# Six staging buffers for the raw weight loads, in place of three, in a two-layer flow trunk

## Chip, cores and metric

The kernel runs on one core of a Trainium2 chip. The metric is the time of one execution in microseconds of device time; the time before is the median of three runs.

## What is computed

Two layers run over 2048 latent tokens and 256 context tokens, each of width 1024 and in fp32. A layer normalises the tokens, projects them with one wide matrix, mixes the columns in four groups of heads, gates the result, projects it back and adds it to the tokens. Cut to what matters here:

```python
def hybrid_layer(x, ctx, c, c_ctx, norm_w, ada_w, ada_b, w_in, w_out, ...):
    shift_l, scale_l, gate_l = jnp.split(jax.nn.silu(c) @ ada_w + ada_b, 3, axis=-1)
    ...
    h_l = rms_norm(x, norm_w) * (1.0 + scale_l[:, None, :]) + shift_l[:, None, :]
    h_c = rms_norm(ctx, norm_w) * (1.0 + scale_c) + shift_c
    pl = split_proj(h_l @ w_in)
    pc = split_proj(h_c @ w_in)
    a_l, a_c = gla_mixer(...)          # chunked gated linear attention, both directions
    b_l = fourier_mix(...)             # 2-D Fourier mixing
    c_l, c_c = swa_mixer(...)          # banded attention with sink logits
    d_l, d_c = na_mixer(...)           # 2-D neighbourhood attention
    y_l = jnp.concatenate([a_l * jax.nn.silu(pl['a_g']), ..., d_l * jax.nn.silu(pl['d_g'])], axis=-1) @ w_out
    x = x + gate_l[:, None, :] * y_l
    ...
```

## The kernel before

**Tiling.** The 2304 tokens are nine subs of 256 (the first is the context). `w_in` is cut into twelve column chunks of 256 (`av`, `aqk`, `cq`, `ckv`, `dk`, `dv`, `dq`, `bv` and the four gates) and one of 32 (`lr`); `w_out` into four chunks of 256. A chunk has eight blocks of 128 rows.

**Precision by halves.** fp32 values are split into a rounded part and the rest, and a product is made of three fp32r matmuls of 128x256 per block (`mm3`, lines 216 to 222): high by high, high by low and low by high. So each weight chunk has to be split on the chip before it is used, and `load_w` (lines 204 to 214) does this. It takes the tiles `hi` (`whi`) and `lo` (`wlo`), of which there are two each, and then four times, for two blocks of rows each: a raw tile `wraw` (three buffers), its load of 256 KB on the SP queue (L211), the cast into `whi` on ACT (L212), and the subtraction into `wlo` (L213), by turns on DVE and POOL. The cast and the subtraction both read the raw tile, and the buffer is free for another load when the subtraction is done. `load_w_lr` (lines 194 to 202) does the same for the narrow chunk with one load, and takes its raw tile from the same buffers. `whi` and `wlo` come free when the last matmul with a chunk is done; with two of each, one chunk is converted while the matmuls use another.

**Stages.** `trunk` goes through the subs three at a time: `first_chunks` (normalise, then `av`, `lr`, `aqk`), `mix_a` (the forward half of the gated linear attention, `gla_fast`, around the chunks `bv`, `ckv`, `dk`, `dv`, and in places the modulation of a later use, `ada`, whose loads `adaw` are multiplied on DVE at L167), then `gla_bwd`, `fnet`, and `attention`, in which attention items alternate with projections of the remaining chunks and with `out_proj` (output projection; its input `y`, 512 KB, is loaded at L1081 into a single buffer, multiplied on DVE at L1083, cast on ACT at L1084). A projection ends with an eviction from PSUM on ACT: a copy (`ev`, L311, L314, L322) or, for the normalised heads, `normrope`, which squares on ACT (`nsq`, L372) and multiplies on DVE (L376). There are two PSUM tiles `ps`/`pso` for all projections, so the matmuls of the projection after next wait for that eviction.

**The start.** `ada_first` computes the first modulation: nine blocks on DVE (`adaw`, L167) and seven as matmuls on PE (`adp`, `pad`, L154), whose result DVE copies at L155 before the first `h` can be made.

**What sets the order.** The instructions of each engine stand in an order that Tile's scheduler fixes when the program is built; each engine then runs its own list in that order, and an instruction that waits holds all that stand behind it on that engine. The DMAs named here are all issued by SP, in one list too. So another number of buffers may move instructions on every engine.

Of the kernel before, what the change touches and what calls it, by code (L numbers as in the profile page):

```python
# [8 lines left out]
F32 = mybir.dt.float32  # L9
# [9 lines left out]
KB = 8  # L19
# [18 lines left out]
class Kern:  # L38
# [155 lines left out]
    def load_w_lr(self, src):  # L194

        nc = self.nc
        w = self.wp.tile([128, KB, 64], F32R, tag="wlr", name="wlr", bufs=1)
        raw = self.wp.tile([128, 2, 256], F32, tag="wraw", name="wraw", bufs=3).rearrange("p a (b n) -> p (a b) n", n=32)[:, 0:KB]
        nc.sync.dma_start(raw, src)
        nc.scalar.copy(w[:, :, 0:32], raw)  # L200
        nc.vector.tensor_tensor(out=w[:, :, 32:64], in0=raw, in1=w[:, :, 0:32], op=ALU.subtract)
        return w, None

    def load_w(self, src):
        nc = self.nc
        lo = self.wp.tile([128, KB, 256], F32R, tag="wlo", name="wlo", bufs=2)
        hi = self.wp.tile([128, KB, 256], F32R, tag="whi", name="whi", bufs=2)
        for i in range(0, KB, 2):
            k = slice(i, i + 2)
            raw = self.wp.tile([128, 2, 256], F32, tag="wraw", name="wraw", bufs=3)  # L210
            nc.sync.dma_start(raw, src[:, k])  # L211
            nc.scalar.copy(hi[:, k], raw)  # L212
            (nc.gpsimd if i % 4 else nc.vector).tensor_tensor(out=lo[:, k], in0=raw, in1=hi[:, k], op=ALU.subtract)  # L213
        return hi, lo
# [1168 lines left out]
```

## Time and profile before

| | before |
|---|---|
| median of 3 runs | 2963.52 us |
| the runs | 2957.93, 2963.52, 2965.28 us |
| the profiled execution | 2951.03 us |
| its span, first to last instruction | 2949.1 us |
| PE busy in it (matmuls) | 2718.3 us, 92% |
| PE weight loads | 2410.2 us, 82% |
| DVE busy | 1609.3 us, 55% |
| ACT busy | 1070.9 us, 36% |
| POOL busy | 837.3 us, 28% |
| mean granted TensorE clock | 0.959 of 2.4 GHz |
| DMA | 458.00 MB, mean 155 GB/s |

The engines run at the same time, so their busy times do not add up. A timeline row gives the start in us, the length in us, the engine, the line, the operation, output and inputs, shapes, the count of merged instructions, and in brackets how long the engine was idle before it and what ended that. `SPq` is SP's issuing of a DMA, not the transfer itself. `PEclk` is the clock granted to TensorE: 1.00 is 2.4 GHz and 0.50 is 1.2 GHz.

### The profile page before, as it was taken

The page shows a single profiled execution, that of the slowest core. Times are in us where ns is not written, and L with a number is a line of the kernel's source. Part 1 is how long each engine was busy: PE and PEld are TensorE (multiplying, and loading weights), DVE is VectorE, ACT ScalarE, POOL GpSimd, SP SyncE. Part 2 cuts the span into 40 slices and gives each one's busy share as a digit, 9 for nine tenths or more (in the row PEclk, how much of TensorE's full clock was granted, in tenths as well). Part 3 has the DMA queues.
Part 4 walks back from the last instruction along what each step waited for, and adds up shares of the span by engine and source line. Part 5 has one row for each costly group of instructions (what it writes and reads, how often), then busy time and mean ns, then how long its engine had stood idle before and what let it go on. Part 6 is the DMA issues. An engine that isn't in the chain of part 4 may idle for free. (4 is left out here: it accounts for less than half of the span.)

```text
span 2949.1 us, 55777 instructions
## 1 busy us (share of the span) xinstructions
PE 2718.3 (92%) x21206; PEld 2410.2 (82%) x21206; DVE 1609.3 (55%) x3741; ACT 1070.9 (36%) x2344; POOL 837.3 (28%) x922
## 2 busy tenths in 40 slices
PE   5989988988999999999959889999879999999998
PEld 5889878976888778887859889889768888878788
DVE  7554775557355454645484553464483646455543
ACT  3333323322344343344224323334232444444432
POOL 3233222234132121312133332332351313121222
PEclk9999988999999999999979999989999999999999
DMA  8635544245565274554464664333465654456545
GB/s 273 194 108 163 169 136 126 84 145 166 162 192 167 81 215 129 158 157 124 147 193 134 196 185 144 93 111 104 119 190 162 199 164 135 146 163 190 161 149 180
DMA packets 476681, 458.00 MB, mean 155 GB/s; under 512 B 54763, under 2 KB 355565, under 8 KB 476013
## 3 DMA queue, kind: packets, MB, share of 16 engines
q1 hardware_dynamic: 472782, 440.66, 48.9%
q0 software_dynamic: 3616, 13.64, 1.9%
q8 instruction: 170, 2.79, 0.4%
q14 instruction: 113, 0.93, 0.1%
HBM read 339.56 MB, written 114.60 MB: 154 GB/s over the span
## 5 line engine op out<-in xcount | busy, mean ns | idle before, releaser
L220 PE MATMUL ps<-whi,hh 128*128 128x256 f32 x1968 | 586.4, 298 | 34.7 <-ACT hh L258 17.2
L222 PE MATMUL ps<-whi,hl 128*128 128x256 f32 x1968 | 582.0, 296 | 10.2 <-DVE hl L259 10.2
L221 PE MATMUL ps<-wlo,hh 128*128 128x256 f32 x1968 | 580.8, 295 | 6.4 <-PEq L639 6.4
L213 POOL TENSOR_TENSOR wlo<-wraw,whi 128x512 fp32r<-128x512 f32 x208 | 280.8, 1350 | 775.7 <-ACT whi L212 735.1
L220 PEld LDWEIGHTS ps<-whi,hh 128*128 128x128 f32 x1968 | 391.9, 199 | 46.4 <-ACT hh L258 19.0
L220 PE MATMUL ps<-hh,whi 128*128 128x256 f32 x1376 | 402.5, 292 | 5.3 <-ACT ev L311 2.3
L222 PEld LDWEIGHTS ps<-whi,hl 128*128 128x128 f32 x1968 | 391.3, 199 | 18.5 <-DVE hl L259 13.9
L221 PE MATMUL ps<-hl,whi 128*128 128x256 f32 x1376 | 403.3, 293 | 0.0
L222 PE MATMUL ps<-hh,wlo 128*128 128x256 f32 x1376 | 402.4, 292 | 0.0
L221 PEld LDWEIGHTS ps<-wlo,hh 128*128 128x128 f32 x1968 | 392.4, 199 | 11.0 <-issue 8.8
L212 ACT CAST whi<-wraw 128x512 fp32r<-128x512 f32 x416 | 242.3, 620 | 378.5 <-DMA wraw<-w_in 206.9
L844 ACT ACTIVATE S<-S,am 128x641 f32<-128x641 f32 (+5 forms) x272 | 226.1, 831 | 339.1 <-DVE am L836 324.5
L220 PE MATMUL pso<-mh,whi 128*128 128x256 f32 x1088 | 316.7, 291 | 5.3 <-DVE xo L1107 2.9
L222 PE MATMUL pso<-mh,wlo 128*128 128x256 f32 x1088 | 316.2, 291 | 2.3 <-POOL wlo L213 1.8
L221 PE MATMUL pso<-ml,whi 128*128 128x256 f32 x1088 | 315.1, 290 | 0.0
L213 DVE TENSOR_TENSOR wlo<-wraw,whi 128x512 fp32r<-128x512 f32 x208 | 187.9, 907 | 170.9 <-ACT whi L212 163.4
L220 PEld LDWEIGHTS ps<-hh,whi 128*128 128x128 f32 x1376 | 265.9, 193 | 15.2 <-issue 7.9
L222 PEld LDWEIGHTS ps<-hh,wlo 128*128 128x128 f32 x1376 | 265.8, 193 | 15.1 <-issue 14.8
L221 PEld LDWEIGHTS ps<-hl,whi 128*128 128x128 f32 x1376 | 266.0, 193 | 11.4 <-issue 11.0
L830 PE MATMUL pse<-kst,q 64*128 64x256 f32 (+2 forms) x1184 | 246.6, 457 | 13.6 <-DVE am L836 12.5
L191 POOL TENSOR_TENSOR rs<-ms,mhalf 128x8 f32<-128x8 f32 (+2 forms) x140 | 171.3, 1226 | 297.5 <-DVE ms L189 288.6
L862 PE MATMUL ppt<-idn,S 128*128 128x128 f32 x1360 | 243.6, 284 | 10.4 <-DVE pt L872 5.2
(203 smaller groups left out, 4866.4 us busy)
## 6 DMA issues: line engine op xcount, KB each, us to landing
wraw<-w_in SPq DMA_DIRECT2D x288, 256.0 KB
wraw<-w_out SPq DMA_DIRECT2D x128, 256.0 KB
adaw<-ada_w SPq DMA_DIRECT2D x82, 256.0 KB
scr_g<-ev SPq DMA_DIRECT2D x68, 256.0 KB
g<-scr_g SPq DMA_DIRECT2D x34, 512.0 KB
y<-scr_y SPq DMA_DIRECT2D x34, 512.0 KB
bias<-nbias SPq DMA_DIRECT2D x48, 256.0 KB
scr_h<-x SPq DMA_DIRECT2D x22, 512.0 KB
```

The lines of the kernel that those rows point to most:

```text
L191: nc.gpsimd.tensor_tensor(out=rs, in0=ms, in1=self.mhalf.to_broadcast([128, n]), op=ALU.pow)
L212: nc.scalar.copy(hi[:, k], raw)
L213: (nc.gpsimd if i % 4 else nc.vector).tensor_tensor(out=lo[:, k], in0=raw, in1=hi[:, k], op=ALU.subtract)
L220: nc.tensor.matmul(out, ah(k), bh(k), start=(k == 0), stop=False)
L221: nc.tensor.matmul(out, ah(k), bl(k), start=False, stop=False)
L222: nc.tensor.matmul(out, al(k), bh(k), start=False, stop=(k == KB - 1))
L830: nc.tensor.matmul(p[:, lo:hi], q[r], k, start=True, stop=True, tile_position=(64 * o, 0))
L844: nc.scalar.activation(out=S[:, 0:w], in_=S[:, 0:w], func=AF.Exp, scale=-1.0, bias=m[:, 0:1], accum_out=m[:, 1:2])
L862: nc.tensor.transpose(p[:, i], S[:, (c0 + i) * 128:(c0 + i + 1) * 128], self.idn)
```

## The change

The raw tile `wraw` has six buffers in place of three, at both places that take one. Nothing else in the source differs; no operation is added or removed, and no size of a tile or a transfer changes.

```diff
@@ def load_w_lr
-        raw = self.wp.tile([128, 2, 256], F32, tag="wraw", name="wraw", bufs=3).rearrange(...)[:, 0:KB]
+        raw = self.wp.tile([128, 2, 256], F32, tag="wraw", name="wraw", bufs=6).rearrange(...)[:, 0:KB]
@@ def load_w
-            raw = self.wp.tile([128, 2, 256], F32, tag="wraw", name="wraw", bufs=3)
+            raw = self.wp.tile([128, 2, 256], F32, tag="wraw", name="wraw", bufs=6)
```

A load into a raw buffer used to wait for the subtraction three raw tiles back, and now waits for the one six back. The order of the instructions changes with it, at these places.

**ACT, first pass over the third to fifth sub, layer 0: the chunk `aqk` (`whi_2312`, raw tiles 2313 to 2325).** Before:

```order
L212 CAST whi_2312<-wraw_2313 128x512
L212 CAST whi_2312<-wraw_2317 128x512
L212 CAST whi_2312<-wraw_2321 128x512
L461 COPY rec_1843<-po_1874 128x256
L432 COPY ktt_1917<-pk_1914 128x256
L258 CAST hh_2329<-x_2331 128x8x128
L231 ACTIVATE sq_2516<-x_2514 128x1024
L450 COPY P_1925<-psl_1926 128x256
L450 COPY P_1925<-psl_1933 128x128
L212 CAST whi_2312<-wraw_2325 128x512
L450 COPY P_1925<-psl_1938 128x128
```

After:

```order
L212 CAST whi_2312<-wraw_2313 128x512
L212 CAST whi_2312<-wraw_2317 128x512
L212 CAST whi_2312<-wraw_2321 128x512
L212 CAST whi_2312<-wraw_2325 128x512
L450 COPY P_1855<-psl_1868 128x128
```

The fourth cast moves up to the third. Over all 104 chunks, the four casts stand in one piece on ACT in 13 of them before and in 78 now; between the third and the fourth there stood 697 ACT instructions in all, and there are 6 now.

**SP, the end of the second pass over subs, layer 0: the loads of the chunk `av` (raw tiles 4532 to 4544) among the `adaw` loads of `ada`.** Before:

```order
L211 DMA wraw_4532<-w_in 128x512
L211 DMA wraw_4536<-w_in 128x512
L164 DMA adaw_4437<-ada_w 128x512
L211 DMA wraw_4540<-w_in 128x512
L164 DMA adaw_4443<-ada_w 128x512
...
L164 DMA adaw_4491<-ada_w 128x512
L320 DMA scr_vd0<-ev_3743 2x64x256 x2
L164 DMA adaw_4497<-ada_w 128x512
L211 DMA wraw_4544<-w_in 128x512
L199 DMA wraw_4549<-w_lr 128x256
```

After:

```order
L164 DMA adaw_4401<-ada_w 128x512
L211 DMA wraw_4540<-w_in 128x512
L211 DMA wraw_4544<-w_in 128x512
L199 DMA wraw_4549<-w_lr 128x256
L211 DMA wraw_4555<-w_in 128x512
L164 DMA adaw_4407<-ada_w 128x512
```

The fourth load of the chunk, 4544, stood behind `adaw_4497` and now stands ahead of `adaw_4407`, sixteen `adaw` loads earlier.

**SP, the start of the program: the last loads of `ada_first` and the first `x` loads.** Before:

```order
L164 DMA adaw_314<-ada_w 128x512
L211 DMA wraw_435<-w_in 128x512
L152 DMA adp_286<-ada_w0 128x1024
L229 DMA x_329<-xin 128x8x128
L229 DMA x_346<-xin 128x8x128
L229 DMA x_363<-xin 128x8x128
L229 DMA x_380<-xin 128x8x128
```

After:

```order
L229 DMA x_329<-xin 128x8x128
L164 DMA adaw_314<-ada_w 128x512
L229 DMA x_346<-xin 128x8x128
L229 DMA x_363<-xin 128x8x128
L229 DMA x_380<-xin 128x8x128
L152 DMA adp_286<-ada_w0 128x1024
```

The last weights for PE's part of the modulation, `adp_286`, stood ahead of four `x` loads of 512 KB and now stand behind them; the raw weight loads of this piece (427, 431, 435) moved to the front of the list.

## Rows read from the trace of the kernel before

**Rows 1.** The page: busy time of the engines, and the chain that ended last, by line.

```profile
PE 2718.3 (92%) x21206; PEld 2410.2 (82%) x21206; DVE 1609.3 (55%) x3741; ACT 1070.9 (36%) x2344; POOL 837.3 (28%) x922
...
PE pse L830 3%; PE ppt L862 3%; PE py L922 2%; PE ps L222 2%; PE ps L220 2%; PE ps L221 2%; DMA y<-scr_y 2%; PE pso L222 1%; PE pso L220 1%; PE pso L221 1%; DMA brec<-scr_so 1%; DMA wraw<-w_out 1%; PE pab L740 0%; DVE wlo L213 0%; DVE y L1083 0%
```

**Rows 2.** Waits, whole span: who waited for whom, total us, times, longest us.

```profile
ACT whi L212 <- DMA wraw<-w_in: 206.9, 75, 12.6
...
ACT whi L212 <- DMA wraw<-w_out: 94.5, 44, 6.0
...
SPq L211 <- DVE wlo L213: 136.8, 92, 10.4
```

**Rows 3.** Timeline of ACT, 396 to 411 us.

```profile
396.71 1.66 ACT L212 CAST whi<-wraw 128x512 fp32r<-128x512 f32 x3
408.99 0.62 ACT L212 CAST whi<-wraw 128x512 fp32r<-128x512 f32 x1 [10.62 <-DMA wraw<-w_in]
...
409.82 0.59 ACT L372 ACTIVATE nsq<-ps 128x512 f32<-128x512 f32 x1
```

**Rows 4.** Timeline of SP, 396 to 406 us.

```profile
404.00 0.33 SPq L211 DMA_DIRECT2D wraw<-w_in  x1
```

**Rows 5.** Timeline of PE at seven places: the instruction behind each gap.

```profile
143.49 0.36 PE L220 MATMUL ps<-whi,hh 128*128 128x256 f32 x1 [3.83 <-DVE nsq L376]
...
222.60 0.80 PE L435 MATMUL pu<-av,ktt 128*128 128x256 f32 x1 [6.66 <-ACT ktt L432]
...
336.45 0.69 PE L430 MATMUL pk<-idn,A 128*128 128x128 f32 x2 [4.25 <-DVE A L422]
...
413.83 0.58 PE L220 MATMUL ps<-whi,hh 128*128 128x256 f32 x1 [4.86 <-DVE nsq L376]
...
1723.51 0.39 PE L220 MATMUL pso<-mh,whi 128*128 128x256 f32 x1 [1.85 <-ACT whi L212]
...
1752.56 0.58 PE L220 MATMUL ps<-hh,whi 128*128 128x256 f32 x1 [2.31 <-ACT ev L311]
...
1896.39 0.38 PE L220 MATMUL ps<-whi,hh 128*128 128x256 f32 x1 [2.51 <-DVE nsq L376]
```

**Rows 6.** Timeline of ACT just before five of those places.

```profile
140.42 0.62 ACT L212 CAST whi<-wraw 128x512 fp32r<-128x512 f32 x1 [10.05 <-DMA wraw<-w_in]
...
217.79 0.62 ACT L212 CAST whi<-wraw 128x512 fp32r<-128x512 f32 x1 [6.36 <-DMA wraw<-w_in]
...
221.23 1.06 ACT L231 ACTIVATE sq<-x 128x1024 f32<-128x1024 f32 x1 [2.38 <-DMA x<-xin]
...
332.41 0.62 ACT L212 CAST whi<-wraw 128x512 fp32r<-128x512 f32 x1 [5.98 <-DMA wraw<-w_in]
...
1750.03 1.99 ACT L212 CAST whi<-wraw 128x512 fp32r<-128x512 f32 x3 [5.26 <-DMA wraw<-w_in]
...
1892.69 0.62 ACT L212 CAST whi<-wraw 128x512 fp32r<-128x512 f32 x1 [8.15 <-DMA wraw<-w_in]
```

**Rows 7.** Timeline of PE in the last projection, 2931 to 2946 us.

```profile
2933.39 0.39 PE L222 MATMUL pso<-mh,wlo 128*128 128x256 f32 x1 [0.84 <-POOL wlo L213]
...
2941.06 0.39 PE L222 MATMUL pso<-mh,wlo 128*128 128x256 f32 x1 [0.85 <-POOL wlo L213]
```

**Rows 8.** Windows: PE, PEld, DVE, ACT, POOL busy; PEclk, DMA share, GB/s.

```profile
0.00:50.00 50.00, 27.04 (x122) 26.40 (x122) 35.55 (x85) 14.06 (x17) 15.97 (x19) 1.00 0.94 318
...
222.00:232.00 10.00, 9.40 (x42) 8.08 (x43) 3.67 (x6) 2.34 (x6) 5.25 (x5) 0.61 0.34 102
336.00:346.00 10.00, 9.09 (x38) 6.76 (x39) 9.27 (x26) 2.35 (x9) 2.40 (x2) 0.50 0.41 132
408.00:418.00 10.00, 5.14 (x28) 4.62 (x26) 8.69 (x21) 1.58 (x4) 4.14 (x3) 0.66 0.38 126
```

**Rows 9.** Timeline of PE, 38 to 46 us: the last part of the modulation.

```profile
39.28 3.57 PE L154 MATMUL pad<-cs,adp 128*128 128x2 f32 x16 [2.48 <-DMA adp<-ada_w]
```

**Rows 10.** Timeline of DVE, 48 to 52 us: the copy of PE's part.

```profile
49.19 0.17 DVE L155 COPY acc<-pad 128x14 f32<-128x14 f32 x1
```

More of the change, by code (lines that the diff above doesn't have):

```diff
@@ L197, in load_w_lr @@
         w = self.wp.tile([128, KB, 64], F32R, tag="wlr", name="wlr", bufs=1)
-        raw = self.wp.tile([128, 2, 256], F32, tag="wraw", name="wraw", bufs=3).rearrange("p a (b n) -> p (a b) n", n=32)[:, 0:KB]
+        raw = self.wp.tile([128, 2, 256], F32, tag="wraw", name="wraw", bufs=6).rearrange("p a (b n) -> p (a b) n", n=32)[:, 0:KB]
         nc.sync.dma_start(raw, src)
```

## The prediction

> **What bounds the kernel now.** I read the page first. PE is busy for 92% of the span and no other engine for more than 55% [rows 1], so what can be won is PE's idle time, some 230 us (2949.1 less 2718.3), and what a lowered clock costs. A change to the weight path matters only where PE waits for it. The direct waits of PE for weights are a few us in all, so by that view alone there is nothing to win.
>
> The list of waits shows something else. ACT's cast of a raw tile waits for the load of that tile 75 times for `w_in` and 44 times for `w_out`, for 206.9 and 94.5 us, 301.4 together [rows 2]. ACT runs its list in order, so during these waits everything behind the cast stands still: the evictions of PSUM, the copies of the linear attention. So I looked, third, at the timeline of ACT around PE's longer gaps.
>
> The place to learn from is 397 to 414 us. Three casts run in a row at 396.71; the fourth starts at 408.99, after 10.62 us of waiting for its load [rows 3]. SP issued that load only at 404.00 [rows 4], because its buffer was one of three and had to be freed by a subtraction first, and because other loads stood ahead of it on SP. Behind the fourth cast, at 409.82, stands the square `nsq` that empties a PSUM tile [rows 3]; PE, which has two of those, waits 4.86 us until 413.83 for the DVE step behind that square [rows 5]. The same picture comes back at 143, 222, 336, 1752 and 1896 us: a cast on ACT that waited for its load for 10.05, 6.36, 5.98, 5.26 and 8.15 us [rows 6], and a PE gap behind it [rows 5]. At 1723 us PE waits for the cast itself, and in the last projection for the last subtraction [rows 5, 7].
>
> **The change, part by part.** No instruction is added or taken out, and no byte. Three things move.
>
> *The fourth load.* With six buffers the load of a chunk's fourth raw tile waits for a subtraction of the chunk before, not of its own chunk. The order shows it: at the place above it goes out sixteen `adaw` loads earlier, and the four casts of a chunk, in one piece in 13 of 104 chunks, are so in 78. So the wait on the fourth load should mostly vanish, and PE's gaps with it, where nothing else is late:
> - 143 us: the gap of 3.83 goes whole; only `nsq` and its DVE step stood behind the cast [rows 5, 6].
> - 414 us: 4.86, whole, for the same reason [rows 3, 5].
> - 222 us: of 6.66 I take half, 3.33. After the cast ACT waited another 2.38 us for an `x` load [rows 5, 6], and that is what is late next.
> - 336 us: of 4.25 half, 2.13: the exponentials behind the cast also need a DVE step whose time I can't separate [rows 5, 6].
> - 1723, 1752 and 1896 us: 1.85, 2.31 and 2.51, whole; nothing else stands between [rows 5, 6].
> - The last projection: 0.84 and 0.85, 1.69 together [rows 7]. There a chunk serves one sub only, and with six buffers the next chunk's loads are issued while the chunk before is still in use.
>
> Together 3.83 + 4.86 + 3.33 + 2.13 + 1.85 + 2.31 + 2.51 + 1.69 = 22.5 us. Bounds: 28.0 if the two halves go whole, 17.1 if they don't go at all.
>
> *The clock.* Behind three of these gaps the granted clock is 0.61, 0.50 and 0.66 over 10 us [rows 8], that is, at 1.2 GHz for part or all of the time, right after PE had stood idle [rows 5]. If PE had work for that time the loss is 3.9 + 5.0 + 3.4 = 12.3 us. Nothing says that one shorter gap keeps the clock up, as other gaps stand near. I take a quarter, 3.1 us; bounds 0 and 12.3.
>
> *A longer burst on ACT.* Four casts in a row in 65 more chunks (78 less 13) hold what is behind them for one more cast: three take 1.66 us and one 0.62, so one more is 0.52 [rows 3], 33.8 us in all. Of ACT's 301.4 us of waiting [rows 2] I traced 22.5 into PE, 7.5%; by that share the longer bursts cost PE 2.5 us. Bounds 0 and 33.8.
>
> *The start.* `adp_286` now stands behind four `x` loads of 512 KB. At the 318 GB/s of the first 50 us [rows 8] these 2.1 MB take 6.6 us. PE's last part ended at 42.85 (39.28 and 3.57) [rows 9] and DVE read it at 49.19 [rows 10], 6.3 us later. So 0.3 us comes through; bounds 0 and 6.6. The DVE work moved ahead of that copy is only taken from behind it.
>
> *SP.* SP's waits for subtractions ahead of a raw load are 136.8 us for DVE's alone [rows 2]. I cost them at nothing: each load still waits for an earlier subtraction, only a longer way back, and behind it on SP stand stores and loads of `x` and `y`, none of which ends one of the gaps in [rows 5]. If that cover is gone, it is the second rival.
>
> The sum: -22.5 - 3.1 + 2.5 + 0.3 = **-22.8 us**. The profiled execution took 2951.03 us (span 2949.1), so by the sum it would take 2928.2. It lies 12.5 us under the median of the runs; against the median, 2963.5, the sum gives **2940.7 us**, which I forecast, a gain of 0.77%. The forecast's own range: at best 28.0 + 12.3 = 40.3 and some 8 more from waits that I did not trace one by one, 2915; at worst 17.1 - 2.5 - 6.6 = 8.0, 2955.
>
> **The rivals.** *The waits only change their name.* Each gap has a second wait close behind the first, as the `x` load at 221 us [rows 6]; the scheduler has filled the waits with other work, and ACT is busy for 36% only. Then no more is left than PE's direct waits for weights, 1.85 + 1.69 = 3.5 us: 2960.0. That the loads hardly come earlier, because SP itself is late, ends here too. Against it stand the places where nothing but the cast's wait separates PE from its work. The Trainium skill (Perfetto Trace Analysis, Identifying the Most-Contended Engine) tells one to work on the most occupied engine first; by that, easing ACT would leave the time where it is. The gaps on PE that end with ACT's late work speak against reading it so here.
>
> *Slower: the raw loads get in front of loads that the chain waits for.* The `y` loads hold 2% of the chain that ended last [rows 1], 59 us. They have one buffer and can't be issued early. With six raw buffers, up to three more loads of 256 KB may be on their way when a `y` load of 512 KB is issued. One of them ahead of each, at an equal rate, makes it half as long again, 29 us; with the traced gain halved (11 us) the time is 2963.5 + 29 - 11 = 2982. It decides from the point where the `y` loads on the chain grow by 22.8/59, 39%, some 200 KB ahead of each. For it: the chain runs through them in every late `out_proj`. Against it: the same bytes pass in the same stages, and the table's mean is 155 GB/s where the first 50 us ran at 318 [rows 8]. The Trainium skill (DMA: Bandwidth & Descriptors, Issuing engines are not separate DMA queues) says that all DMAs run on the same 16 engines and interleave; by it every load sent earlier takes from those under way. No row of before shows how much.
>
> **How the numbers follow.** About 0.3%, 9 us, is what a measurement of this kernel can tell from no change. The forecast has a chance of 0.62; the first rival 0.24, within 0.3%; the second 0.14. So faster 0.62, same 0.24, slower 0.14. A range from 2915 to 2968 takes in the forecast's own range but for a twentieth at its lower end, and the first rival with 4 us above the median; the second rival is left out.
>
> **What would show it.** Right: ACT's wait for `wraw` falls from 301 us to under 100; at the four places in layer 0 the fourth cast follows the third within a us; PE's gaps before L220 that end with `nsq` shrink; the last projection has no wait for `wlo`. Wrong in the first way: ACT's wait falls, but PE's idle time stays near 230 us, with other releasers. Wrong in the second: the chain's share of `y` loads rises, and DVE's wait for them. If ACT's wait for `wraw` stays near 300 us, the premise is wrong.

## The result and the profile after

The time is **2922.72 us** (median of 4 runs, 2912.85 to 2926.31), against 2961.47 us for the kernel before (4 runs, 2957.93 to 2965.28). The ratio is **0.9878, 95% interval 0.9851 to 0.9904**: faster by 1.2%, 36 us at 2961, where 22.8 us were forecast. The medians themselves lie 38.75 us apart. The sign is as forecast and the time is in the range, but the gain is more than half as large again as the sum, and the runs below show that it came only partly for the reasons given.

The profiled execution took 2924.73 us (span 2922.9), 26.3 less than that of before. This pair shows less than the medians, since the profiled execution of before lies 10 us under its median and that of after 2 us above. From the page of after, busy time and the chain by line, for [rows 1]; below it the core's span and mean granted clock, which were 2949.1 us and 0.959 before:

```profile
PE 2702.4 (92%) x21206; PEld 2404.3 (82%) x21206; DVE 1619.6 (55%) x3741; ACT 1066.4 (36%) x2344; POOL 865.5 (30%) x922
...
PE pse L830 3%; PE ppt L862 3%; PE py L922 2%; PE ps L222 2%; PE ps L220 2%; PE ps L221 2%; DMA y<-scr_y 2%; PE pso L222 1%; PE pso L220 1%; PE pso L221 1%; PE pab L740 1%; DMA wraw<-w_out 0%; DVE ml L1085 0%; DVE S L836 0%; DVE y L1083 0%
```

```profile
core 0: 2922.9 us, clock 0.963
```

PE's idle time (span less busy) went from 230.8 to 220.5 us, only 10.3 less; the other 15.9 us is PE's busy time, for the same 21206 matmuls. Busy time shrinks when more of it runs at 2.4 GHz: a mean of 0.959 over 2949.1 us is (1 - 0.959) x 2 x 2949.1 = 242 us at 1.2 GHz, and 0.963 over 2922.9 us is 216. Where PE has work, half of such time is loss, so by this estimate the clock gives back some 13 us between these two executions (the four of after have 0.960 to 0.964). The Trainium skill (Perfetto Trace Analysis, Identifying the Most-Contended Engine) says that the matmul busy share is not a good measure of how close a kernel is to its roofline; here it stayed at 92% while the time fell by 26 us.

The waits, total us, times, longest us. First ACT's after the change, for [rows 2]:

```profile
ACT wlr L200 <- DMA wraw<-w_lr: 20.5, 5, 6.3
ACT whi L212 <- DMA wraw<-w_in: 14.0, 10, 2.7
ACT whi L212 <- DMA wraw<-w_out: 0.3, 1, 0.3
```

Then two of DVE and PE, before:

```profile
DVE y L1083 <- DMA y<-scr_y: 96.5, 29, 5.5
...
PE ps L220 <- DVE nsq L376: 16.8, 10, 4.9
```

and after:

```profile
DVE y L1083 <- DMA y<-scr_y: 101.6, 28, 6.5
...
PE ps L220 <- DVE nsq L376: 23.5, 11, 9.4
```

ACT's wait for raw tiles of `w_in` and `w_out` fell from 301.4 to 14.3 us, as forecast (the narrow chunk's, at L200, rose from 3.0 to 20.5). But PE's waits for the `nsq` step, which should have shrunk, grew: 16.8 us before, 23.5 after. So 287 us less waiting on ACT stand beside 10.3 us less idling on PE, and the question is whether these waits had anything to do with the gain.

Where the 26 us are, place by place (times of before; a place ends after at the same count of matmuls; us before and after): 138 to 254 us, 116 to 103; 714 to 813, 99 to 92; 1835 to 1951, 116 to 106; from 2848 to the last matmul, 97 to 89. In between some is given back: 1061 to 1150, 89 to 94; 1400 to 1619, 219 to 224; and 2761 to 2848, 87 to 93. The largest piece, of before and then of after (PE, PEld, DVE, ACT, POOL busy; PEclk, DMA share, GB/s):

```profile
138.00:254.00 116.00, 102.19 (x740) 94.52 (x740) 72.27 (x189) 42.43 (x103) 44.22 (x40) 0.90 0.41 126
```

```profile
138.00:241.00 103.00, 94.24 (x746) 88.41 (x745) 71.80 (x174) 42.35 (x98) 42.44 (x40) 0.97 0.45 137
```

Five us of these 13 are PE's idle time (13.8 before, 8.8 after); the rest is busy time, and goes with the clock, 0.90 against 0.97.

### The profile page after: what moved, and what is told of

Same layout as the page of the kernel before. It is cut to its first block, busy times and chain, and to the rows that moved or that the text cites. A ratio compares the mean times of both kernels' runs of the same rounds, so it can differ in the third digit from the quotient of the medians.

```text
span 2922.9 us, 55816 instructions
## 1 busy us (share of the span) xinstructions
PE 2702.4 (92%) x21206; PEld 2404.3 (82%) x21206; DVE 1619.6 (55%) x3741; ACT 1066.4 (36%) x2344; POOL 865.5 (30%) x922
## 5 line engine op out<-in xcount | busy, mean ns | idle before, releaser
L213 POOL TENSOR_TENSOR wlo<-wraw,whi 128x512 fp32r<-128x512 f32 x208 | 304.8, 1478 | 580.0 <-ACT whi L212 520.7
L221 PEld LDWEIGHTS ps<-wlo,hh 128*128 128x128 f32 x1968 | 394.7, 201 | 12.3 <-issue 9.2
L221 PE MATMUL ps<-hl,whi 128*128 128x256 f32 x1376 | 396.9, 288 | 0.0
L212 ACT CAST whi<-wraw 128x512 fp32r<-128x512 f32 x416 | 230.5, 618 | 142.6 <-PE ps L221 43.2
L213 DVE TENSOR_TENSOR wlo<-wraw,whi 128x512 fp32r<-128x512 f32 x208 | 200.7, 972 | 130.3 <-ACT whi L212 118.0
```

The costliest lines, as they stand in the source:

```text
L221: nc.tensor.matmul(out, ah(k), bl(k), start=False, stop=False)
```

## The experiments

All ratios are to runs of the kernel before on the same chip. Idle (span less PE busy time), clock and ACT's wait (for raw tiles, `w_in` and `w_out`) are those of the one profiled execution.

| kernel | ratio, 95% interval | PE idle us | clock | ACT's wait us |
|---|---|---|---|---|
| before | 1 | 230.8 | 0.959 | 301.4 |
| six (the change) | 0.9878, 0.9851 to 0.9904 | 220.5 | 0.963 | 14.3 |
| two (e1) | 1.0113, 1.0082 to 1.0143 | 251.7 | 0.957 | 425.7 |
| four (e2) | 0.9832, 0.9797 to 0.9866 | 199.8 | 0.963 | 43.4 |
| five (e3) | 0.9907, 0.9876 to 0.9938 | 212.9 | 0.961 | 30.5 |
| six, fourth load in its own chunk (e4) | 0.9907, 0.9878 to 0.9936 | 209.6 | 0.963 | 254.6 |
| six, order of three (e5) | 0.9961, 0.9946 to 0.9975 | 221.3 | 0.957 | 274.3 |
| six, order of two (e6) | 1.0028, 1.0016 to 1.0041 | 234.3 | 0.956 | 368.9 |
| six, order of four (e7) | 0.9802, 0.9782 to 0.9821 | 196.3 | 0.966 | 35.7 |
| three, unrelated reordering (e8) | 0.9989, 0.9977 to 1.0002 | 223.4 | 0.955 | 311.1 |
| six, order of three, SP free (e9) | 0.9916, 0.9892 to 0.9939 | 218.4 | 0.957 | 4.6 |
| six, PE's order of three (e10) | 1.0036, 1.0016 to 1.0056 | 245.4 | 0.954 | 14.2 |
| six, order of four, SP free (e11) | 0.9830, 0.9805 to 0.9854 | 197.5 | 0.963 | 16.7 |
| as e9, less modulation work on DVE (e12) | 0.9868, 0.9847 to 0.9890 | 205.2 | 0.962 | 3.5 |

### How many buffers: two, four, five

Only the number changes, at both places:

```diff
-name="wraw", bufs=6
+name="wraw", bufs=2
```

(and 4, and 5).

> Two raw buffers: the third and the fourth load of a chunk now wait for subtractions of their own chunk. Theory A (what the change took away is ACT standing still in front of a cast whose load waits for its own chunk): ACT's wait for raw loads rises above the 301 us of three buffers, to 400 to 600, and the time by the 7 to 13% of it that reached PE, 10 to 30 us over the kernel before (2971 to 2991). Theory B (the gain is only another order of the instructions, a matter of luck): ACT's wait may rise, the time falls anywhere within 15 us of the kernel before.

> Four raw buffers: all four loads of the next chunk have room, nothing beyond it. Theory A: this is where the gain sits; ACT's wait for raw loads falls under 60 us and the time to within 8 us of six buffers (2915 to 2931). Theory C (depth: every buffer more brings loads earlier, and the gain grows with it): a third of the gain, 2948, half the steps between 301 and the 14 us or so of six. Theory B: anywhere between 2920 and 2975.

> Five raw buffers. Theory A: as four and six, 2915 to 2931, ACT's wait for raw loads under 40 us. Theory C: two thirds of the gain, 2935. Theory B: no order among four, five and six; they differ from each other by 10 us or more.

Two buffers are slower by 33 us, with 124 us more of ACT's wait; theory A had 10 to 30 us. Four hold the whole gain and come out faster than A had them, which speaks against depth (C). But five, run beside four on the same chip, are 0.75% behind it, where A wanted them equal; six, run earlier, lies between, its interval overlapping with both. Neither A nor C explains that: 10 us or more between four and five without an order is what theory B expected.

### The fourth load waits in its own chunk, with six buffers

```diff
-            raw = self.wp.tile([128, 2, 256], F32, tag="wraw", name="wraw", bufs=6)
-            nc.sync.dma_start(raw, src[:, k])
+            raw = r0 if i == 6 else self.wp.tile([128, 2, 256], F32, tag="wraw", name="wraw", bufs=6)
+            r0 = raw if i == 0 else r0; nc.sync.dma_start(raw, src[:, k])
```

> Six buffers, but the fourth load of each chunk goes into the tile of the chunk's first load, so that it waits for a subtraction of its own chunk as with three buffers, while the first three loads of two chunks have room. Theory A: ACT's wait for raw loads stays near 301 us (250 to 350), and the time near the kernel before (2950 to 2970). Theory C: the depth gives most of the gain, 2925 to 2940. Theory B: anywhere between 2920 and 2975.

ACT's waits of this kernel:

```profile
ACT whi L212 <- DMA wraw<-w_in: 174.2, 66, 11.6
ACT whi L212 <- DMA wraw<-w_out: 80.4, 25, 7.1
```

The wait stayed, as A said (254.6 us), and 731 ACT instructions stand between third and fourth casts (697 before). Yet the ratio is 0.9907. So theory A, the prediction's own, fell in its plain form: ACT can stand still for 255 us and three quarters of the gain is there. The time, 2925 us, is at the edge of what C gave, but C had failed at four and five. What e4 shares with the others is another order of the instructions on all engines.

### Waits and order taken apart

Each of these kernels is first built with one number of buffers, and the order of every engine's instructions is recorded; then it is built with six, and each instruction gets an edge to its forerunner on the same engine that fixes the order and adds no wait. For the order of three:

```diff
+def _program(arrays, raw, order=None):
...
+        Kern(nc, tc, aps, raw=raw).build()
+        if order:
+            ins = {i.name: i for i in nc.cur_bb.bb.instructions}
+            dep = mybir.DependencyInfo(mybir.DependencyClass.NoSync, mybir.DependencyReason.DATA)
+            for names in order.values():
+                names = [x for x in names if x in ins]
+                for a, b in zip(names, names[1:]):
+                    tc.add_manual_dep(ins[b], a, dep, reason="order")
...
+    nc = _program(arrays, 6, _order(_program(arrays, 3)))
```

Two and four have 2 or 4 in the last line. The control keeps three raw buffers:

```diff
-name="T", bufs=2
+name="T", bufs=3
...
-name="sbe", bufs=2
+name="sbe", bufs=3
```

> Six raw buffers, but every engine is held to the order of instructions that it has with three buffers: only the waits for the buffers are shorter. Theory W (the shorter waits themselves are the gain, as the prediction has it): at least two thirds of the gain, a ratio to the kernel before of 0.992 or less (some 2937 for 2961). Theory O (the waits that went cost next to nothing, and the gain is the other order): a ratio of 0.997 or more, though ACT's wait for raw loads falls below 250 us.

> Six raw buffers, held to the order of instructions that belongs to two buffers, a kernel that took 1.0113 of the time before. Theory W: the order costs nothing, the waits do; the ratio falls to that of six buffers, 0.990 or less. Theory O: the order is the loss; the ratio stays over 1.006.

> Six raw buffers, held to the order that belongs to four (0.9832 of the time before). Theory O: the order of four is simply a better one than that of six; the ratio stays at 0.981 to 0.985. Theory W: with the waits of six the ratio is that of six, 0.988, whatever the order; or, if four was fast by its shorter queue of loads in flight, it goes back to 0.988.

> Three raw buffers as before; a third buffer for two small tiles that the weights do not touch (the table tile T of the Fourier stage and the state tile sbe of the backward attention), which makes the scheduler put 2077 PE, 581 DVE, 300 ACT and 282 SP instructions in another place. Theory W: next to nothing, ratio 0.997 to 1.003, as ACT's 301 us of waiting stay. Theory O: another order is another time; a ratio outside 0.995 to 1.005 would show that a reordering alone can be worth half of the gain or more.

With the waits of six in all of them, the orders of two, three, six and four give 1.0028, 0.9961, 0.9878 and 0.9802. The spread between orders, 2.3%, is larger than the whole effect of the change. That is theory O, with a reserve: these orders hold SP's too, so that ACT's waits differ with them (368.9, 274.3, 14.3 and 35.7 us). Not every order moves the time, however: the control moved 2077 PE instructions and brought 0.1%, with 1 inside its interval. It is one such order; how far others would scatter is not shown. And shorter waits in an unchanged order do bring something, 0.4% with three and 0.85% with two (1.0113 to 1.0028), each between the two expectations. In e5 ACT still waits 274.3 us, because SP too was held to its order, and the fourth load stands as late in it as before. So a next step was needed.

### Loads early, work in place

In e9 only SP is free, in e10 only PE is held; e11 is e9 with the order of four:

```diff
-    nc = _program(arrays, 6, _order(_program(arrays, 3)))
+    order = _order(_program(arrays, 3))
+    nc = _program(arrays, 6, {e: v for e, v in order.items() if "SP" not in e})
```

> Six raw buffers; PE, ACT, DVE and POOL are held to their order of three buffers, and only SP may issue in another order (406 of its instructions move), so that the raw loads can go out early while no work on an engine is moved. Theory L (what costs is ACT standing still for late loads): ACT's wait for raw loads falls from 301 us under 100, and the ratio to 0.988 to 0.992. Theory O (what counts is the order of the work on the engines): the wait falls too, but the ratio stays within 0.003 of the 0.9961 that six buffers in the full order of three gave.

> Six raw buffers; PE alone is held to its order of three buffers, the other engines and SP are free, so that the four casts of a chunk stand together on ACT in 78 of 104 chunks as after the change. Theory O in the form that PE's order is what counts: the ratio stays at that of the run in which only SP is free. In the form that the order of ACT, DVE and POOL counts: the ratio falls to that of the change, 0.988. Theory L: no difference from the run in which only SP is free, which by it has nearly the whole gain already.

> Six raw buffers; the engines are held to the order of four buffers, SP is free, so that the loads can go out as early as six buffers allow. Theory O: as the full order of four with six buffers, 0.9802, within 0.003. Theory L: ACT's wait for raw loads is 36 us there already, so that little is left: 0.977 to 0.980. A slower time, 0.984 or more, would say that raw loads sent early hold up other loads.

e9 is the change as the prediction thought of it: loads early, and not one PE instruction in another place. ACT's wait falls to 4.6 us and the ratio to 0.9916, in the span that theory L named, some 25 us of 2955. In steps: shorter waits 0.4%, loads issued earlier another 0.45%, the engines' own order another 0.4% to the 0.9878 of the change; the intervals of the last two overlap by 0.0012, so that the third step is likely rather than certain. e10 shows that the engines' orders belong together: PE in the order of three, with ACT, DVE and POOL in one made for six, is slower than before, although ACT waits 14.2 us only. None of its expectations named that. PE idles 14.6 us more than before, 9.2 of it at one place, where it waited 0.19 us before and here waits for DVE's `bsq` of the backward attention:

```profile
2187.83 0.66 PE L677 MATMUL pyt<-idn,bsq 128*128 128x128 f32 x2 [9.38 <-DVE bsq L673]
```

In e11 loads sent still earlier brought nothing (0.9830 against 0.9802, with overlapping intervals). With SP free (e9 and e11; in the change the order is the scheduler's own) and ACT's wait down to 4.6, 14.3 and 16.7 us, the orders of three, six and four thus give 0.9916, 0.9878 and 0.9830: 0.9% by the order of the engines' work.

Because e9 has PE's order of before, its gaps can be laid beside those of [rows 5] one by one. At the four places of layer 0 they were 3.83, 6.66, 4.25 and 4.86 us, and are in e9:

```profile
142.17 0.36 PE L220 MATMUL ps<-whi,hh 128*128 128x256 f32 x1 [2.89 <-DVE nsq L376]
...
222.22 2.08 PE L435 MATMUL pu<-av,ktt 128*128 128x256 f32 x4 [7.66 <-ACT ktt L432]
...
335.12 0.69 PE L430 MATMUL pk<-idn,A 128*128 128x128 f32 x2 [3.41 <-DVE A L422]
...
407.20 0.58 PE L220 MATMUL ps<-whi,hh 128*128 128x256 f32 x1 [5.32 <-DVE nsq L376]
```

Of 19.6 us, 19.3 are still there. The later ones went: 1.85 and 2.51 whole, 2.31 to 0.56, the `wlo` waits of the last projection whole. The four gaining places of the change say the same: in e9 the first takes 117 us (116 before), and the others 95, 112 and 91 (99, 116 and 97 before). Now the place to learn from, 407 us, in e9; ACT first:

```profile
389.62 2.18 ACT L212 CAST whi<-wraw 128x512 fp32r<-128x512 f32 x4
391.70 0.41 ACT L200 CAST wlr<-wraw 128x256 fp32r<-128x256 f32 x1
394.90 0.60 ACT L372 ACTIVATE nsq<-ps 128x512 f32<-128x512 f32 x1 [2.79 <-PE ps L222]
```

and DVE:

```profile
396.20 0.75 DVE L167 CUSTOM_DVE_ANT_0 adaj<-adaw,csb,ada 128x512 f32<-128x512 f32 x1 [4.72 <-DMA adaw<-ada_w]
...
403.56 0.69 DVE L167 CUSTOM_DVE_ANT_0 adaj<-adaw,csb 128x512 f32<-128x512 f32 x1 [1.78 <-DMA adaw<-ada_w]
...
405.12 0.68 DVE L374 TENSOR_REDUCE ss<-nsq 128x8 f32<-128x512 f32 x1
...
406.46 0.69 DVE L376 TENSOR_TENSOR nsq<-ps,wdq 128x512 f32<-128x512 f32 x1
```

The four casts run in one piece and `nsq`, the square, is done at 395.5, but DVE comes to its sum `ss` only at 405.12 (the scaled sum `ms` and the multiplication follow): its list holds the multiplications of `ada` ahead of it, and they wait for their own loads. PE waits as before. This could be read in the trace of before, on the engine that the prediction didn't look at. DVE at the steps behind the late casts, 141, 411 and 1893 us:

```profile
141.63 0.42 DVE L374 TENSOR_REDUCE ss<-nsq 128x4 f32<-128x256 f32 x1 [0.98 <-ACT nsq L372]
...
408.44 0.69 DVE L167 CUSTOM_DVE_ANT_0 adaj<-adaw,csb 128x512 f32<-128x512 f32 x1 [1.79 <-DMA adaw<-ada_w]
...
409.94 1.28 DVE L201 TENSOR_TENSOR wlr<-wraw,wlr 128x256 fp32r<-128x256 f32 x1 [0.80 <-ACT wlr L200]
...
411.76 0.68 DVE L374 TENSOR_REDUCE ss<-nsq 128x8 f32<-128x512 f32 x1
...
1893.65 1.29 DVE L201 TENSOR_TENSOR wlr<-wraw,wlr 128x256 fp32r<-128x256 f32 x1 [7.66 <-ACT wlr L200]
```

The bracket says how long DVE stood idle for ACT: 0.98 us at 141; 0.80 at 409.94 and none at 411.76, where the longer wait close by was for `adaw` (1.79); 7.66 at 1893. By so much at most can that DVE instruction come earlier if ACT alone is earlier. e9 gave 0.94 at the first place, nothing at the second, and the whole 2.51 us at the third.

### DVE's modulation work taken away

As e9, built in the same recorded order; then

```diff
-                nc.vector.tensor_tensor_reduce(out=j, in0=w, in1=csb[:, s, cc], scale=1.0,
+                nc.vector.tensor_tensor_reduce(out=j[:, 0:n], in0=w[:, 0:n], in1=csb[:, s, c * 512:c * 512 + n], scale=1.0,
```

with `n` 8 in place of 512 but for the first modulation: the kernel leaves out the other 504 columns of each product.

> As the run in which only SP is free (six raw buffers, the engines in their order of three), with one thing taken off DVE: in the modulation of a later use each of the DVE multiplications by adaw takes 8 of its 512 columns, so that this modulation is not the one wanted; loads and the number of instructions stay. In the run with full columns PE still waited 2.9, 7.7, 3.4 and 5.3 us at the four layer 0 places of the prediction, though ACT no longer waited for raw loads. Theory D (there DVE, busy with these multiplications and waiting for their loads, is late right behind ACT): the first, third and fourth gap fall under 1.5 us each, the second stays over 5, for it waits for an x load; some 10 us less, a ratio of 0.988. Theory N (the cause is elsewhere): the gaps stay within a us and the ratio within 0.002 of 0.9916.

PE at these places:

```profile
110.78 2.08 PE L491 MATMUL pz<-decx,lrt 65*128 65x256 f32 x4 [2.06 <-DMA lrt<-scr_lr]
...
143.59 0.28 PE L220 MATMUL ps<-whi,hh 128*128 128x256 f32 x1
...
221.22 2.08 PE L435 MATMUL pu<-av,ktt 128*128 128x256 f32 x4 [8.01 <-ACT ktt L432]
...
331.18 0.44 PE L430 MATMUL pk<-idn,A 128*128 128x128 f32 x2 [0.59 <-DVE A L422]
...
400.47 0.58 PE L220 MATMUL ps<-whi,hh 128*128 128x256 f32 x1 [5.73 <-DVE nsq L376]
```

The third gap fell from 3.41 to 0.59, and the second stayed at 8.01 (ACT's square in front of it waits for an `x` load). That is theory D. The first gap is gone too, but not for D's reason. DVE's step there, in e9 and then in e12, came only 0.27 us earlier:

```profile
141.61 0.42 DVE L376 TENSOR_TENSOR nsq<-ps,wck 128x256 f32<-128x256 f32 x1
```

```profile
141.34 0.42 DVE L376 TENSOR_TENSOR nsq<-ps,wck 128x256 f32<-128x256 f32 x1
```

PE came to this place late, at 143.59 where in e9 it went on at 142.17: it had waited 2.06 us for `lrt` at 110.78, and then ran at a lower clock (0.66 over 110 to 120 us). So the first place decides nothing. The fourth gap did not fall, against D, and DVE shows why:

```profile
399.50 0.23 DVE L167 CUSTOM_DVE_ANT_0 adaj<-adaw,csb,ada 128x8 f32<-128x8 f32 x1 [6.32 <-DMA adaw<-ada_w]
399.65 0.17 DVE L189 TENSOR_SCALAR ms<-ss 128x8 f32<-128x8 f32 x1
399.73 0.68 DVE L376 TENSOR_TENSOR nsq<-ps,wdq 128x512 f32<-128x512 f32 x1
```

There it is not the work but its load: a multiplication stands between `ss` and `ms` and waits 6.32 us for `adaw`. The ratio is 0.9868, with the expected 0.988 inside its interval; one gap of 2.8 us does not make the step of some 14 us from e9, and how much of it comes from less DVE work elsewhere (1613.2 us busy in e9, 1551.2 here) isn't separated.

The fastest kernel of the study is e7, six buffers in the order of four: 0.9802, 2899 us. Its lead over plain four (0.9832) lies within their intervals; its lead over the change (0.9878) does not, so the scheduler's own order for six is not the best one found.

## Why the prediction came out as it did

- **The premise held.** ACT's wait fell to 14.3 us (forecast: under 100), and in the trace of after the four casts of most chunks run in one piece.
- **That the early loads are worth about what the sum said is luck in good part.** Against 22.5 us of direct gaps, e9 shows 25 us by its ratio and 15.4 between the two profiled executions; but at the nine places only 9.6 us came back, and 1.5 us went again where two of the gaps grew. The terms 3.83 and 4.86 ("go whole; only `nsq` and its DVE step stood behind the cast") are the step that failed: e9 gave 0.94 and nothing. The halves taken at 222 and 336, 3.33 and 2.13, gave nothing and 0.84. Thus 14.2 us of the sum stood on places where DVE, or an `x` load, was late right behind ACT, the very thing that the first rival said. (Of these only the gap at 336 us was shown to shrink when DVE is eased, in e12.) The terms of 1723 to 1896 (6.67) and of the last projection (1.69) hold: 6.1 and 1.7. All of PE's idle time fell by 12.4 us in e9. The rest of e9's gain is spread over places that the prediction did not trace, such as the `brec` waits of the backward attention and 784 us, where PE waited 1.62 us for a cast.
- **The order was not priced.** The prediction said that three things move and costed only those. All engines were reordered, and that brought, likely, the part of the gain beyond e9. The gaps at 143 and 222 us are gone in the change and not in e9: between 62 and 199 us PE has no gap over 1.5 us after the change. But it then waits 3.24, 1.55 and 1.43 us at 199 to 203, for `hh`, `rb` and `hl`, and 4.03 us at 326 for `nsq`, where it waited 4.25 at 336.
- **The clock** was sized at 3.1 us of 12.3. By the profiled executions it gave some 13 in the change and nothing in e9 (0.957). But that one is e9's slowest; the other five have 0.960 or 0.961, against a median of 0.959 in the 17 runs of before beside them, which is some 5 us. So some of it needs no new order, and some does: the stretch from 138 us ran at 0.97 in place of 0.90 in the change, and at 0.88 in e9, which kept the gaps. That fits the cause that the prediction gave, PE standing idle. e12 shows it both ways, in 110 to 120 us, where PE newly waited 2.06, and in 140 to 150, where its gap was gone; e9 and then e12:

```profile
110.00:120.00 10.00, 10.00 (x80) 9.81 (x79) 3.56 (x6) 7.33 (x8) 2.47 (x2) 1.00 0.90 320
140.00:150.00 10.00, 7.56 (x50) 7.29 (x51) 8.32 (x26) 0.66 (x2) 1.02 (x1) 0.83 0.67 219
```

```profile
110.00:120.00 10.00, 9.22 (x44) 8.63 (x45) 2.71 (x9) 2.45 (x3) 1.97 (x2) 0.66 0.94 328
140.00:150.00 10.00, 10.00 (x86) 10.00 (x85) 4.20 (x35) 1.22 (x4) 1.70 (x2) 1.00 0.85 282
```

- **New waits.** The change has one of 9.41 us where before had 4.86. After the change, DVE and then PE:

```profile
390.18 0.68 DVE L374 TENSOR_REDUCE ss<-nsq 128x8 f32<-128x512 f32 x1
394.32 0.69 DVE L167 CUSTOM_DVE_ANT_0 adaj<-adaw,csb 128x512 f32<-128x512 f32 x1 [3.46 <-DMA adaw<-ada_w]
...
394.94 0.17 DVE L189 TENSOR_SCALAR ms<-ss 128x8 f32<-128x8 f32 x1
395.01 0.68 DVE L376 TENSOR_TENSOR nsq<-ps,wdq 128x512 f32<-128x512 f32 x1
```

```profile
395.75 0.58 PE L220 MATMUL ps<-whi,hh 128*128 128x256 f32 x1 [9.41 <-DVE nsq L376]
```

  ACT's `nsq` ended there at 381.2; DVE again was behind with `ada`, and SP sent four raw loads among the `adaw` loads that DVE waits for. SP, after the change:

```profile
386.20 1.15 SPq L211 DMA_DIRECT2D wraw<-w_in  x1
387.47 0.45 SPq L164 DMA_DIRECT2D adaw<-ada_w  x1
387.97 1.40 SPq L211 DMA_DIRECT2D wraw<-w_in  x3
```

- **Longer bursts, +2.5:** not seen, and not tried by itself; the worst end of the forecast's own range took in these 2.5 us and not their bound of 33.8. **The start, +0.3:** DVE's copy of PE's part waited 1.31 us for it, at 55.19, and the first 138 us of work took 1.2 us longer.
- **The first rival** (the waits only change their name) is right, but for 0.94 and 0.84 us, at four of the nine places and wrong as a whole: easing ACT, which is busy for 36% only, took 0.84% off in e9 with all work in place. PE's idle time, 220.5, is near the 230 that the prediction named as its sign; what it left out is that PE's busy time can fall as well.
- **The second rival** did not come: DVE's wait for `y` rose from 96.5 to 101.6 us (101.8 in e9), 5 us where 29 were priced. The Trainium skill (DMA: Bandwidth & Descriptors, Issuing engines are not separate DMA queues) says that DMAs run on the same 16 DMA engines and interleave; that may be in these 5 us, but no run here separates it.

## What to carry to other kernels

A wait on one engine is worth at most what the next engine stands idle for it: follow the chain one step further, and read the bracket of the instruction behind the wait before its gap is booked (0.98, 0.80 and 7.66 us here fit the outcome of three places; they were read after the runs, and no further place was foretold by them). Where a scheduler places the instructions, a buffer count is an order as well; building the changed kernel in the old order takes the two apart. And it pays to try the neighbouring counts: four buffers did at least as well as six, with fewer.

## What the runs showed that was not expected

The same work with the same buffers took between 0.9802 and 1.0036 of the time before, by the order alone, SP's among them (e5 to e7, e9 to e11 and the change). PE's order of three among orders made for six (e10) cost 1.6% against the change, with PE's idle time up from 220.5 to 245.4 us.
